# A two-layer decoder trunk: the second pair of gate and up columns computed conventionally

## The chip, the core and the metric

The kernel runs on one core of a Trainium2 chip. Its engines are called as the profile calls them: PE is TensorE (matmuls; PEld its weight loads), DVE is VectorE, ACT is ScalarE, POOL is GpSimd, SP is SyncE, which here only issues DMAs. The metric is the device time of one execution in microseconds; smaller is better.

## The reference

The input is 512 tokens of 1024 features in float32. Two layers run one after the other, each `x += 1/2 SwiGLU(RMSNorm(x)); x += Mixer(RMSNorm(x)); x += 1/2 SwiGLU(RMSNorm(x))`. The mixer of the first layer is pooling beside latent attention, that of the second a gated short convolution; the change doesn't touch them. The four SwiGLU half-steps are what it touches:

```python
def swiglu(x, w_gate, w_up, w_down):        # (512,1024) @ (1024,2816), twice; then @ (2816,1024)
    return (jax.nn.silu(x @ w_gate) * (x @ w_up)) @ w_down
```

## The kernel before

**Precision.** Activations and weights are split into a high and a low float32r part (`split`, lines 86 to 88: ACT casts the high part, DVE subtracts for the low one), and each product is three matmuls: high by high, high by low, low by high. Tiles `whi` and `wlo` hold the two parts of one weight chunk of 128 by 1024, each with three buffers; so the split of a chunk can be made when the matmuls on the third chunk before it are done.

**Layout.** Features lie in partitions, tokens in the free dimension. The 2816 hidden columns are 22 tiles of 128, taken as 11 pairs, numbered 0 to 10. A pair needs gate and up for two column tiles.

**Seven products.** Pairs 1 to 10 are computed by a Strassen-Winograd scheme on 2 by 2 blocks: two halves of the 1024 features by two halves of the 512 tokens on the activation's side. Instead of eight block products there are seven, P1 to P7, each of 24 matmuls 256 columns wide. Each product takes one combination of the weights, made by DMAs that add into a loaded tile (POOL's queue, tiles `sto` and `ar`; plain loads go through SP's queue), and one combination of the normalised input, a *factor*: `B11`, `T1`, `N2`, `B21`, `T3`, `N22`, `T4`. Pairs are computed in a staggered order, so that the P4 of one pair comes behind the P5 and P1 of the next. Their results sit in PSUM banks (six, tag `bank`), are copied or combined by ACT and DVE (`gate_up`), gated, and turned into blocks `hh` for the down projection, which also goes by seven products (`down`), in three groups of pairs.

**The start of a half-step.** The factors need the normalised input, and so the reciprocal norm R of each token, which is known late. Pair 0 is therefore computed conventionally from the input scaled by the gains alone, tile `xs`, and R is multiplied in afterwards. That is four chunks, each a `quarter` of 24 matmuls 512 columns wide. Between them the squares are summed over the partitions (`token_sums`, line 316), turned into R (`rsqrt`, DVE), spread over the partitions by matmuls (`norm_rows`, line 334) and copied by ACT (line 336). Then DVE makes the normalised tiles `xn` (line 379), DVE and ACT the seven factors (lines 382 to 405; the T4 is last), and behind them the gating of pair 0 (lines 453 to 464) and its blocks.

**What sets the order.** The text is written pair by pair, but a scheduler decides in which order the instructions stand in each engine's queue; within a queue an instruction waits for all ahead of it. Weight chunks are split three ahead of their use and loaded up to six ahead, through three buffers `raw`, through `sto` and `ar` (two each) for the summed ones.

Of the kernel before, what the change touches and what calls it, by code (L numbers as in the profile page):

```python
# [10 lines left out]
F32 = mybir.dt.float32  # L11
F32R = mybir.dt.float32r
AF = mybir.ActivationFunctionType
# [28 lines left out]
def trunk(ctx: ExitStack, tc: tile.TileContext, a, out):  # L42
# [21 lines left out]
    def bank(tag="bank", bufs=None):  # L64
        return pp.tile([P, 512], F32, tag=tag, name=tag, bufs=bufs)
# [101 lines left out]
    for l in range(2):  # L167
        for f in ("ffn1", "ffn2"):
            if f == "ffn2":
                if l == 0:  # L170
                    chunks += [Chunk(a["a_lat"][j], CH) for j in range(5)]
                    chunks += [Chunk(a["a_kr"], NK * DR)]
                    chunks += [Chunk(a["a_u"][j], CH) for j in reversed(range(4))]
                    chunks += [Chunk(a["a_w_out"][j, :, :CH // 2], CH // 2) for j in range(NK)]
                    chunks += [Chunk(a["a_w_out"][j, :, CH // 2:], CH // 2) for j in range(NK)]
                else:
                    for j in range(NK):
                        chunks += [Chunk(a["c_w_in"][s * NK + j], CH) for s in (1, 2, 0)]
                    chunks += [Chunk(a["c_w_out"][j], CH) for j in range(NK)]
            gu = a[f + "_w_gu"][l]  # L180
            turn = len(plans) + 1
            chunks += [Chunk(gu[0, q], CH) for q in (0, 2, 1, 3)]

            what = []
            for gi, (p0, p1) in enumerate(GROUPS):
                last = gi + 1 == len(GROUPS)
                what += [("gu", p) for p in range(max(p0, 1), p1 + 1 - last) if ("gu", p) not in what]
                what += [("down", (gi, e)) for e in range(2)]
            units = []
            for kind, p in what:  # L190
                if kind == "gu":
                    units.append(seven([gu[p, q] for q in range(4)], CH, turn))
                else:
                    gi, e = p
                    p0, p1 = GROUPS[gi]
                    n = 2 * (p1 - p0) * P
                    w = a[f"{f}_w_down{gi}"][l]
                    units.append(seven([w[e, q] for q in range(4)], n, turn))
            order = staggered([k for k, _ in what], max(j for j, (k, _) in enumerate(what) if k == "gu"))
            plans[l, f] = what, order  # L200
            chunks += [units[i][s] for i, s in order]
# [138 lines left out]
    def ffn(l, f, which, after, first=False):  # L340
        what, order = plans[l, f]
        with ExitStack() as es:
# [6 lines left out]
            def eight():  # L349
                return fp.tile([P, 8, HT], F32, tag="hz", name="hz")  # L350
# [17 lines left out]
            norm = lambda: rows.extend(norm_rows(norm_columns()))  # L368
            quarter(banks[2:4], 0, True, False, None if first else norm)
            if first:  # L370
                norm()
            R, Rp = rows
            with tc.tile_pool(name="np", bufs=1) as np_:
                xn = [np_.tile([P, 4, T], F32, tag=f"xn{e}", name=f"xn{e}") for e in range(2)]
# [29 lines left out]
                factor("N22", b22, -1.0)  # L404
                nc.vector.scalar_tensor_tensor(t1, t1, -1.0, b21, ALU.mult, ALU.subtract)
                factor("T4", t1)
            quarter(banks[0:2], 4, False, True)
            quarter(banks[2:4], 4, False, True)


# [7 lines left out]
            def put(p, names, src):  # L418

                j, c = home[p % 4][names[0]]  # L420
                j += 7 * (p // 4)
                if j not in four:
                    if j in (0, 1, 2, 7, 9, 10, 14):
                        t = hx.tile([P, 4 * T + 64], F32R, tag="hx", name="hh")[:, 48:48 + 4 * T]
                    else:
                        t = hy.tile([P, 4 * T], F32R, tag="hy", name="hh")
                    four[j] = t.rearrange("p (c f t) -> p c f t", c=2, f=4)
                v = four[j][:, :, c:c + len(names)]
                split(src, v[:, 0], v[:, 1])
                hfac.setdefault(p, {}).update({b: (v[:, 0, i], v[:, 1, i]) for i, b in enumerate(names)})  # L430
# [3 lines left out]
            def blocks(p, hz, rest):  # L434
# [11 lines left out]
                else:  # L446
                    nc.vector.scalar_tensor_tensor(hz[:, T4], hz[:, N2], -1.0, hz[:, B21], ALU.mult, ALU.subtract)
                    put(p, ("B21", "T4"), hz[:, B21:T4 + 1])


            hz = eight()
            for e in range(2):
                g, u = banks[2 * e:2 * e + 2]
                t = tp.tile([P, T], F32, tag="t", name="t")
                nc.vector.tensor_mul(t, g, R)  # L455
                nc.scalar.activation(t, t, AF.Silu)
                v = tp.tile([P, T], F32, tag="t", name="v")
                nc.vector.tensor_mul(v, u, R)
                if e == 0:
                    nc.vector.tensor_mul(hz[:, B11], v[:, :HT], t[:, :HT])  # L460
                    nc.vector.tensor_mul(hz[:, B12], v[:, HT:], t[:, HT:])
                else:
                    nc.vector.tensor_mul(hz[:, B21], v[:, :HT], t[:, :HT])
                    nc.vector.scalar_tensor_tensor(hz[:, N22], v[:, HT:], -1.0, t[:, HT:], ALU.mult, ALU.mult)


            live = {}
# [86 lines left out]

            for n, (i, s) in enumerate(order):
                if n == 3:
                    blocks(0, hz, False)
                    blocks(0, hz, True)
                kind, p = what[i]
                (gate_up if kind == "gu" else down)(i, p, s)  # L560

# [489 lines left out]
```

## Time and profile before

| | us |
|---|---|
| runs, median of 3 | 1764.47 |
| lowest and highest | 1763.59, 1764.65 |
| the profiled execution, its own time | 1768.79 |
| its span, first to last instruction | 1767.0 |
| PE busy | 1697.0 |
| DVE busy | 1328.1 |
| ACT busy | 906.9 |
| POOL busy | 312.0 |

The profiled execution is one more run, with the profiler on; its times start with its first instruction. The half-steps' conventional pairs end on PE at 40, 578, 928 and 1447 us. The mean granted clock of TensorE over the span is 0.985 of full speed.

### The profile page before, as it was taken

How to read it: one execution, taken by the hardware profiler on the slowest of the kernel's cores; microseconds unless marked ns; L12 is line 12 of the kernel's file. 1: busy time of each engine (PE TensorE's matmuls, PEld its weight loads, DVE VectorE, ACT ScalarE, POOL GpSimd, SP SyncE). 2: the span in 40 equal slices, each digit the busy share in tenths (PEclk: the TensorE clock that was granted, in tenths of full speed). 3: DMA queues.
4: the chain of work that ended last, by engine and by line, in shares of the span. 5: the costliest groups of instructions: out<-in, count | busy, mean ns of one | idle time of the engine just before them, and what ended most of it. 6: DMA issues, size and time to landing. Idle time of an engine off the chain costs nothing.

```text
span 1767.0 us, 31319 instructions
## 1 busy us (share of the span) xinstructions
PE 1697.0 (96%) x12642; PEld 1594.4 (90%) x12642; DVE 1328.1 (75%) x1891; ACT 906.9 (51%) x1300; POOL 312.0 (18%) x359
## 2 busy tenths in 40 slices
PE   7899999999999799999998999999999989999998
PEld 5799999978888799999988999999788879999998
DVE  6877786877896977677798777868755677867866
ACT  5654554564654554564556545545322345645553
POOL 2111111224202111111121111112100111111111
PEclk9999999998999899999999999999999999999999
DMA  6689888740015498889776899897322248988986
GB/s 215 157 209 215 216 211 212 165 142 24 19 42 173 106 214 218 213 206 217 173 194 153 208 219 223 207 212 164 108 96 96 96 133 194 222 216 209 218 210 138
DMA packets 89185, 303.19 MB, mean 172 GB/s; under 512 B 10704, under 2 KB 11472, under 8 KB 89040
## 3 DMA queue, kind: packets, MB, share of 16 engines
q0 software_dynamic: 36864, 130.04, 42.1%
q1 hardware_dynamic: 50512, 169.89, 27.2%
q8 instruction: 99, 1.62, 0.4%
q10 hardware_dynamic: 1664, 1.26, 0.2%
q14 instruction: 46, 0.38, 0.1%
HBM read 299.06 MB, written 2.10 MB: 170 GB/s over the span
## 4 chain that ended last, share of the span: by engine, by line
PE 80%; DVE 10%; issue 3%; ACT 3%; DMA 3%; POOL 1%; SPq 0%; ACTq 0%; DVEq 0%; POOLq 0%
PE bank L476 61%; PE bank L218 5%; PE bank L219 5%; PE bank L220 5%; DMA sto<-in_ffn_w_gu 2%; DVE wlo L88 2%; ACT whi L87 1%; DVE xn L379 1%; DVE xs L242 1%; DVE fT L88 1%; DVE fB L88 1%; PE bank L882 0%; PE held L218 0%; PE held L219 0%; PE held L220 0%
## 5 line engine op out<-in xcount | busy, mean ns | idle before, releaser
L476 PE MATMUL bank<-hh,whi 128*128 128x256 f32 x2464 | 429.9, 278 | 7.3 <-ACT whi L87 3.9
L476 PEld LDWEIGHTS bank<-hh,whi 128*128 128x128 f32 x2464 | 374.3, 188 | 10.4 <-ACT whi L87 4.9
L476 PE MATMUL bank<-fT,whi 128*128 128x256 f32 x1920 | 337.8, 279 | 8.5 <-ACT whi L87 2.9
L476 PE MATMUL bank<-hh,wlo 128*128 128x256 f32 x1232 | 341.5, 278 | 4.1 <-DVE wlo L88 4.1
L87 ACT CAST whi<-sto 128x1024 fp32r<-128x1024 f32 (+1 forms) x192 | 196.1, 1023 | 263.7 <-PE bank L476 164.4
L88 DVE TENSOR_TENSOR wlo<-sto,whi 128x1024 fp32r<-128x1024 f32 (+1 forms) x192 | 228.8, 1192 | 107.4 <-ACT whi L87 106.1
L476 PEld LDWEIGHTS bank<-fT,whi 128*128 128x128 f32 x1920 | 292.1, 189 | 11.2 <-ACT whi L87 3.5
L476 PE MATMUL bank<-fT,wlo 128*128 128x256 f32 x960 | 266.7, 278 | 0.0
L476 PE MATMUL bank<-fN,whi 128*128 128x256 f32 x1280 | 237.5, 288 | 14.4 <-ACT x L482 9.5
L476 PEld LDWEIGHTS bank<-hh,wlo 128*128 128x128 f32 x1232 | 231.0, 188 | 4.9 <-DVE wlo L88 4.9
L476 PE MATMUL bank<-fB,whi 128*128 128x256 f32 x1280 | 231.3, 280 | 4.2 <-DVE t L455 4.1
L476 PEld LDWEIGHTS bank<-fN,whi 128*128 128x128 f32 x1280 | 199.3, 193 | 25.3 <-ACT x L482 13.6
L87 ACT CAST whi<-a 128x1024 fp32r<-128x1024 f32 (+1 forms) x128 | 131.3, 1026 | 144.4 <-PE bank L476 88.1
L476 PEld LDWEIGHTS bank<-fB,whi 128*128 128x128 f32 x1280 | 197.8, 190 | 4.9 <-DVE t L455 4.9
L124 POOL DMA_DIRECT2D sto<-in_ffn_w_gu x120 | 104.6, 871 | 517.3 <-DVE wlo L88 294.9
L88 DVE TENSOR_TENSOR wlo<-a,whi 128x1024 fp32r<-128x1024 f32 (+1 forms) x128 | 152.3, 1190 | 53.3 <-ACT whi L87 53.0
L88 DVE TENSOR_TENSOR wlo<-ar,whi 128x1024 fp32r<-128x1024 f32 (+1 forms) x128 | 152.3, 1190 | 49.1 <-ACT whi L87 48.8
L87 ACT CAST whi<-ar 128x1024 fp32r<-128x1024 f32 (+1 forms) x128 | 130.9, 1022 | 112.2 <-PE bank L476 55.6
L476 PE MATMUL bank<-fN,wlo 128*128 128x256 f32 x640 | 181.3, 283 | 6.2 <-DVE wlo L88 6.2
L476 PE MATMUL bank<-fB,wlo 128*128 128x256 f32 x640 | 178.7, 279 | 5.5 <-DVE wlo L88 5.5
L476 PEld LDWEIGHTS bank<-fT,wlo 128*128 128x128 f32 x960 | 181.3, 189 | 0.0
L219 PE MATMUL bank<-xs,whi 128*128 128x512 f32 x392 | 154.9, 395 | 1.8 <-DVE xs L242 1.6
(242 smaller groups left out, 2877.9 us busy)
## 6 DMA issues: line engine op xcount, KB each, us to landing
sto<-in_ffn_w_gu POOLq DMA_DIRECT2D x120, 512.0 KB, 7.4
a<-in_ffn_w_gu SPq DMA_DIRECT2D x80, 512.0 KB, 6.5
sto<-in_ffn_w_down POOLq DMA_DIRECT2D x48, 512.0 KB, 7.7
sto<-in_ffn_w_gu SPq DMA_DIRECT2D x40, 512.0 KB, 4.2
ar<-in_ffn_w_gu SPq DMA_DIRECT2D x40, 512.0 KB, 5.4
ar<-in_ffn_w_gu POOLq DMA_DIRECT2D x40, 512.0 KB, 5.4
a<-in_ffn_w_down SPq DMA_DIRECT2D x32, 512.0 KB, 6.0
raw<-in_c_w_in SPq DMA_DIRECT2D x24, 512.0 KB, 3.4
```

The lines of the kernel that those rows point to most:

```text
L87: nc.scalar.copy(hi, raw)
L88: nc.vector.tensor_sub(lo, raw, hi.bitcast(F32))
L124: nc.gpsimd.dma_start(out=self.unit[tag], in_=self.srcs[q], accum_op=ALU.add)
L218: nc.tensor.matmul(ps, wh, ah, start=start, stop=False)
L219: nc.tensor.matmul(ps, wh, al, start=False, stop=False)
L220: nc.tensor.matmul(ps, wl, ah, start=False, stop=stop)
L242: nc.vector.scalar_tensor_tensor(xl, x[k], g, xh.bitcast(F32), ALU.mult, ALU.subtract)
L379: nc.vector.scalar_tensor_tensor(xn[e][:, i], x[k], gains[:, which, k:k + 1], R if e else Rp, ALU.mult, ALU.mult)
L476: nc.tensor.matmul(o, w_[:, s], a_, start=fresh and e == 0 and k == 0 and i == 0, stop=last and i == 2, skip_group_check=True)
```

## The change

Pair 1 is computed as pair 0 is: from the scaled input, conventionally, in four quarters. Its chunks are plain loads in the order of its two column tiles, so its first two quarters complete the first tile's gate and up, the last two the second's. In the text its quarters stand behind the gating of pair 0, and the blocks of pair 0 are made between them. The gating of pair 0 becomes a function, `first_h`, which serves both. The products begin with pair 2. Two smaller edits go along. In the first half-step the norm's steps move from behind the second quarter into the third, which for that goes ahead of the factors. And the hidden blocks of pairs 0 and 1 now live in pool `hy`, those of the next two in pool `hx`, since `hx` holds the scaled input for longer.

```diff
-            chunks += [Chunk(gu[0, q], CH) for q in (0, 2, 1, 3)]
+            chunks += [Chunk(gu[p, q], CH) for p in range(2) for q in ((0, 1, 2, 3) if p else (0, 2, 1, 3))]
...
-                what += [("gu", p) for p in range(max(p0, 1), p1 + 1 - last) if ("gu", p) not in what]
+                what += [("gu", p) for p in range(max(p0, 2), p1 + 1 - last) if ("gu", p) not in what]
...
             quarter(banks[2:4], 0, True, False, None if first else norm)
             if first:
-                norm()
+                quarter(banks[0:2], 4, False, True, norm)
...
-            quarter(banks[0:2], 4, False, True)
+            if not first:
+                quarter(banks[0:2], 4, False, True)
             quarter(banks[2:4], 4, False, True)
...
-                    if j in (0, 1, 2, 7, 9, 10, 14):
+                    if j in (4, 5, 6, 7, 9, 10, 14):
...
+            hz = first_h(banks)
+            pair1 = [bank() for _ in range(2)]
+            quarter(pair1[0:2], 0, True, False)
+            quarter(pair1[0:2], 4, False, True)
+            blocks(0, hz, False)
+            blocks(0, hz, True)
+            pair1 += [bank() for _ in range(2)]
+            quarter(pair1[2:4], 0, True, False)
+            quarter(pair1[2:4], 4, False, True)
+            hz = first_h(pair1)
...
                 if n == 3:
-                    blocks(0, hz, False)
-                    blocks(0, hz, True)
+                    blocks(1, hz, False)
+                    blocks(1, hz, True)
```

On DVE in the second half-step (the third looks the same) these rows stand around the last factor, `fT4`; `wlo` from `sto` or `a1` are low halves for products, `t`, `v` and `hz` belong to the gating of pair 0. Before:

```order
L88 TENSOR_TENSOR fT3_6296<-hz_6403,fT3_6296 128x1024
L405 SCALAR_TENSOR_TENSOR hz_6403<-hz_6403,xn1_6396 128x1024
L455 TENSOR_TENSOR t_6489<-bank_6299,R_6378 128x512
L458 TENSOR_TENSOR v_6492<-bank_6300,R_6378 128x512
L88 TENSOR_TENSOR fT4_6298<-hz_6403,fT4_6298 128x1024
L88 TENSOR_TENSOR wlo_6508<-sto_6303,whi_6507 128x1024
L460 TENSOR_TENSOR hz_6488<-v_6492,t_6489 128x256
L461 TENSOR_TENSOR hz_6488<-v_6492,t_6489 128x256
L88 TENSOR_TENSOR wlo_6538<-a1_6425,whi_6537 128x1024
```

And now, where `raw_6241` and `raw_6332` are the chunks of pair 1's third and fourth quarter:

```order
L88 TENSOR_TENSOR fT3_6204<-hz_6310,fT3_6204 128x1024
L405 SCALAR_TENSOR_TENSOR hz_6310<-hz_6310,xn1_6303 128x1024
L456 TENSOR_TENSOR t_6397<-bank_6207,R_6285 128x512
L459 TENSOR_TENSOR v_6400<-bank_6208,R_6285 128x512
L88 TENSOR_TENSOR fT4_6206<-hz_6310,fT4_6206 128x1024
L88 TENSOR_TENSOR wlo_6416<-raw_6241,whi_6415 128x1024
L461 TENSOR_TENSOR hz_6396<-v_6400,t_6397 128x256
L462 TENSOR_TENSOR hz_6396<-v_6400,t_6397 128x256
L88 TENSOR_TENSOR wlo_6444<-raw_6332,whi_6443 128x1024
```

The low halves for two products at that place gave way to those for the third and fourth quarter of pair 1; what stands ahead of them is as it was.

In the last half-step the place ahead of `fT4` differs; before:

```order
L88 TENSOR_TENSOR fT3_15397<-hz_15504,fT3_15397 128x1024
L405 SCALAR_TENSOR_TENSOR hz_15504<-hz_15504,xn1_15497 128x1024
L88 TENSOR_TENSOR wlo_15558<-ar_15407,whi_15557 128x1024
L455 TENSOR_TENSOR t_15590<-bank_15400,R_15479 128x512
L88 TENSOR_TENSOR fT4_15399<-hz_15504,fT4_15399 128x1024
L458 TENSOR_TENSOR v_15593<-bank_15401,R_15479 128x512
L88 TENSOR_TENSOR wlo_15609<-sto_15404,whi_15608 128x1024
L460 TENSOR_TENSOR hz_15589<-v_15593,t_15590 128x256
```

And now (`raw_15124` is pair 1's second quarter, `raw_15154` its third):

```order
L88 TENSOR_TENSOR fT3_15117<-hz_15223,fT3_15117 128x1024
L405 SCALAR_TENSOR_TENSOR hz_15223<-hz_15223,xn1_15216 128x1024
L88 TENSOR_TENSOR wlo_15279<-raw_15124,whi_15278 128x1024
L456 TENSOR_TENSOR t_15310<-bank_15120,R_15198 128x512
L88 TENSOR_TENSOR fT4_15119<-hz_15223,fT4_15119 128x1024
L459 TENSOR_TENSOR v_15313<-bank_15121,R_15198 128x512
L88 TENSOR_TENSOR wlo_15329<-raw_15154,whi_15328 128x1024
L461 TENSOR_TENSOR hz_15309<-v_15313,t_15310 128x256
```

Here it is the second quarter's low half that stands between the subtraction for T4 (line 405) and `fT4`, where a product's stood.

On PE in the first half-step the token sums (line 316) and the matmuls that spread R (line 334) stand elsewhere, among the wide matmuls of the third quarter; this is the difference, first for the sums:

```order
 L219 MATMUL bank<-xs_162,whi 128x512
 L220 MATMUL bank<-xs_162,wlo 128x512
+L316 MATMUL held<-ones,acc 128x2 x3
 L218 MATMUL bank<-xs_151,whi 128x512
 L219 MATMUL bank<-xs_151,whi 128x512
 L220 MATMUL bank<-xs_151,wlo 128x512
-L334 MATMUL held<-ident,rb 128x128 x4
 L218 MATMUL bank<-xs_151,whi 128x512
```

then for the spreading matmuls:

```order
 L218 MATMUL bank<-xs_162,whi 128x512
 L219 MATMUL bank<-xs_162,whi 128x512
+L334 MATMUL held<-ident,rb 128x128 x4
 L220 MATMUL bank<-xs_162,wlo 128x512
 L218 MATMUL bank<-xs_162,whi 128x512
```

The last three token sums moved behind twelve wide matmuls, and the spreading matmuls stand eight wide ones behind them.

## Rows read from the trace of the kernel before

**Rows 1.** The page's part 1: busy time, share of the span, instructions.

```profile
PE 1697.0 (96%) x12642; PEld 1594.4 (90%) x12642; DVE 1328.1 (75%) x1891; ACT 906.9 (51%) x1300; POOL 312.0 (18%) x359
```

**Rows 2.** Busy us and instructions by engine in three stretches; PEclk, DMA.

```profile
932.00:936.00 4.00, 1.70 (x14) 1.42 (x12) 4.00 (x5) 2.25 (x3) 0.00 (x0) 1.00 0.35 70
936.00:940.00 4.00, 1.43 (x6) 1.00 (x5) 4.00 (x6) 2.96 (x3) 0.00 (x0) 0.52 0.00 0
940.00:944.00 4.00, 4.00 (x25) 4.00 (x25) 4.00 (x7) 0.68 (x2) 0.87 (x1) 0.63 0.63 100
```

**Rows 3.** TensorE's timeline, half-step 1: start, us, line, tiles.

```profile
37.70 0.39 PE L218 MATMUL bank<-xs,whi 128*128 128x512 f32 x1
...
40.42 0.28 PE L476 MATMUL bank<-fT,whi 128*128 128x256 f32 x1
...
41.92 0.39 PE L476 MATMUL bank<-fT,whi 128*128 128x256 f32 x2
...
43.28 0.39 PE L476 MATMUL bank<-fT,whi 128*128 128x256 f32 x2
```

**Rows 4.** The same view where the first pair ends, half-steps 2 to 4.

```profile
577.30 0.39 PE L220 MATMUL bank<-xs,wlo 128*128 128x512 f32 x1
...
927.51 0.40 PE L476 MATMUL bank<-fT,whi 128*128 128x256 f32 x2
...
1446.50 0.40 PE L476 MATMUL bank<-fT,whi 128*128 128x256 f32 x2
```

**Rows 5.** VectorE's timeline, line 529 in the four half-steps.

```profile
119.42 0.42 DVE L529 SCALAR_TENSOR_TENSOR hz<-bank,c 128x256 f32<-128x256 f32 x1
...
662.15 0.42 DVE L529 SCALAR_TENSOR_TENSOR hz<-bank,c 128x256 f32<-128x256 f32 x1
...
963.55 0.42 DVE L529 SCALAR_TENSOR_TENSOR hz<-bank,c 128x256 f32<-128x256 f32 x1
...
984.65 0.42 DVE L529 SCALAR_TENSOR_TENSOR hz<-bank,c 128x256 f32<-128x256 f32 x1
...
1004.47 0.42 DVE L529 SCALAR_TENSOR_TENSOR hz<-bank,c 128x256 f32<-128x256 f32 x1
...
1524.68 0.42 DVE L529 SCALAR_TENSOR_TENSOR hz<-bank,c 128x256 f32<-128x256 f32 x1
```

**Rows 6.** VectorE's timeline: the first normalised tiles, two low halves behind them.

```profile
33.72 1.41 DVE L379 SCALAR_TENSOR_TENSOR xn<-x,gains,held 128x512 f32<-128x512 f32 x2 [2.02 <-ACT R L336]
...
574.11 1.40 DVE L379 SCALAR_TENSOR_TENSOR xn<-x,gains,held 128x512 f32<-128x512 f32 x2
...
918.11 1.41 DVE L379 SCALAR_TENSOR_TENSOR xn<-x,gains,held 128x512 f32<-128x512 f32 x2
...
938.23 1.22 DVE L88 TENSOR_TENSOR wlo<-sto,whi 128x1024 fp32r<-128x1024 f32 x1
...
1435.50 0.75 DVE L379 SCALAR_TENSOR_TENSOR xn<-x,gains,held 128x512 f32<-128x512 f32 x1 [1.93 <-ACT R L336]
...
1453.28 1.22 DVE L88 TENSOR_TENSOR wlo<-ar,whi 128x1024 fp32r<-128x1024 f32 x1
```

**Rows 7.** TensorE's timeline: the token sums, half-steps 1 and 4.

```profile
27.91 0.72 PE L316 MATMUL held<-ones,acc 128*128 128x2 f32 x6
...
1430.72 0.95 PE L316 MATMUL held<-ones,acc 128*128 128x2 f32 x8
```

**Rows 8.** Timelines of TensorE and ScalarE on the way to R, half-step 2.

```profile
566.42 1.05 PE L334 MATMUL held<-ident,rb 128*128 128x128 f32 x8
...
571.88 1.05 ACT L87 CAST whi<-sto 128x1024 fp32r<-128x1024 f32 x1 [8.44 <-DMA sto<-in_ffn_w_gu]
...
572.96 0.59 ACT L336 COPY R<-held 128x512 f32<-128x512 f32 x1
```

**Rows 9.** TensorE's waits: us in total, times, longest.

```profile
PE bank L476 <- ACT x L482: 11.2, 13, 3.2
```

**Rows 10.** The page's part 6: DMA issues, KB each, median us to landing.

```profile
sto<-in_ffn_w_gu POOLq DMA_DIRECT2D x120, 512.0 KB, 7.4
```

More of the change, by code (lines that the diff above doesn't have):

```diff
@@ L448, in blocks, with first_h @@
                     put(p, ("B21", "T4"), hz[:, B21:T4 + 1])
[L451 to L464, printed above, removed]
+            def first_h(banks):
+                hz = eight()
+                for e in range(2):
+                    g, u = banks[2 * e:2 * e + 2]
+                    t = tp.tile([P, T], F32, tag="t", name="t")
+                    nc.vector.tensor_mul(t, g, R)
+                    nc.scalar.activation(t, t, AF.Silu)
+                    v = tp.tile([P, T], F32, tag="t", name="v")
+                    nc.vector.tensor_mul(v, u, R)
+                    if e == 0:
+                        nc.vector.tensor_mul(hz[:, B11], v[:, :HT], t[:, :HT])
+                        nc.vector.tensor_mul(hz[:, B12], v[:, HT:], t[:, HT:])
+                    else:
+                        nc.vector.tensor_mul(hz[:, B21], v[:, :HT], t[:, :HT])
+                        nc.vector.scalar_tensor_tensor(hz[:, N22], v[:, HT:], -1.0, t[:, HT:], ALU.mult, ALU.mult)
+                return hz
+            hz = first_h(banks)
[8 more added lines that the diff above has]
+            hz = first_h(pair1)
             live = {}
```

## The prediction

> **What bounds the kernel now.** I read the page first. TensorE is busy for 96% of the span [rows 1], so what can be won is only what TensorE loses, and what a change adds to its work is paid in full unless it fills such a loss. The table of stretches then showed where it loses: not in the middle of the half-steps but just behind the four places where the conventional first pair ends and the first seven-product pair begins. There VectorE is busy without a break while TensorE stands, and after it has stood the granted clock drops to its lower level, 1.2 GHz: in the third half-step TensorE is busy for 1.70 and 1.43 us of two neighbouring stretches of 4 us, and the granted clock is 0.52 and then 0.63 in the stretches that follow [rows 2].
>
> The timeline of TensorE gives the size of its work. Twelve 512-wide matmuls of the conventional pair take 40.42 - 37.70 = 2.72 us, 0.2267 us each; twelve 256-wide ones of a product take 43.28 - 41.92 = 1.36 us, 0.1133 each [rows 3]. A pair computed conventionally is 96 wide matmuls, 21.76 us; by seven products it is 168 narrow ones, 19.04 us; one product is 2.72 us.
>
> Two marks per half-step measure the loss. E is where the conventional pair ends on TensorE: 40.42, 577.53 (the last start, 577.30, and one spacing), 927.51 and 1446.50 [rows 3, 4]. The other mark is VectorE's instruction on line 529, which comes once in a pair, behind its last product, P4. For the third pair computed by products it stands at 119.42, 662.15, 1004.47 and 1524.68 [rows 5]. From E to there it takes **79.00, 84.62, 76.96 and 78.18 us**. Bare work would be nine products to the first P4 (order: P5, P1, P6, P2, P7, next P5, P3, next P1, P4), 24.5 us, and twice 19.0 more: 62.6. So 14 to 22 us are lost each time.
>
> What is late is VectorE's chain that makes the factors. It begins with the normalised tiles, at a time that I call T0: 33.72, 574.11, 918.11, 1435.50 [rows 6]. In the third half-step the low half of T4 is done and the next weights' low half ends at 938.23 + 1.22 = 939.45, T0 + 21.3 [rows 6], while E was 9.4 us behind T0. TensorE has nothing to do for that time but the few products whose factors are ready.
>
> **The change part by part.** *Added work.* 21.76 - 19.04 = 2.72 us of TensorE in each half-step, 10.9 in all, certain.
>
> *Cover.* The 21.76 us of the second conventional pair stand between E and the first product. They need no factor, only the scaled input and weights. The cover ends where something else on VectorE is late, and the order shows what: the low half of the third quarter of the new pair stands behind the low half of T4. In the first three half-steps it ends at T0 + 21.3 (the same instructions in the same number stand ahead of it as ahead of the row at 938.23). TensorE wants it two quarters behind E, at E + 10.88. So TensorE waits 10.4 - (E - T0).
>
> - Half-step 1: three of four token sums move behind 12 more wide matmuls, 27.91 + 2.72 = 30.6, and from the sums to T0 it takes 1435.50 - 1430.72 = 4.8 us where nothing is in between [rows 6, 7], so T0 is 35.4. TensorE reaches the transposing matmuls 8 wide ones behind the sums, 1.8 us, and their operand comes some 1 us later (4.8 less the 1.05 and 0.6 of matmuls and copy is about 3): E becomes 41.4. The wait is 10.4 - 6.0 = 4.4 us.
> - Half-step 2: T0 was late, because the copy of R at 572.96 stood on ScalarE behind a cast whose summed weights landed only at 571.88, though the matmuls for it began at 566.42 [rows 8]. Now a plain load stands there. R follows the matmuls (1.05) and a cast, T0 becomes about 568.5, and the wait is 10.4 - 9.0 = 1.4. If the plain load lands no sooner than the summed one, T0 stays at 574.1 and the wait is 7.
> - Half-step 3: E - T0 is 9.4, the wait 1.0.
> - Half-step 4: here the order puts the second quarter's low half behind the subtraction for T4. That place is 1453.28 in the old trace, the operation ends at 1454.5 [rows 6], and TensorE wants it at E + 5.44 = 1451.9: wait 2.5.
>
> *Clock.* What TensorE does at the lower level costs the same time again. The nearest row is the third half-step's pair of waits [rows 2]: 1.43 x 0.48 + 4 x 0.37 = 2.2 us. No stall of the size of 1.0 to 1.4 has to do that. I take 2.2 for the wait of 4.4, 1.5 for that of 2.5, nothing for the others; the bounds are nothing, and 2.2 in each half-step for this wait and once more for the one that comes next.
>
> *The first product pair.* With all factors ready it still has waits of its own. P6 adds into the bank of P1, so ScalarE must first copy P1's result (the waits for that copy sum to 11.2 us over the kernel, the longest 3.2 [rows 9]). Ahead of that copy stands a cast into the buffer that P1 frees: 1.05 and 0.59 [rows 8], 1.7 us of TensorE. Then an estimated 1.7 us for the subtraction ahead of P3 and for the last cast and gating behind P4. From the end of the pair to line 529: 24.5 + 3.4 = 28 us. In half-steps 2 and 3 the summed weights of P6 come late as well: their accumulation is issued when P5's low half is made, by the order some 5 us behind the third quarter's, about T0 + 26, and takes 7.4 us to land [rows 10], so T0 + 33.4, 1.2 us later than the cast could begin: 29.2.
>
> *The second product pair*, then the third of all. Before, the pair behind the first one took 984.65 - 963.55 = 21.1 us, and the next 19.8 [rows 5]. I let the second one behind the start cost 21.1 now too.
>
> *Not on the path.* A pair less by products is three weight splits less on ScalarE and VectorE, four loads and four accumulations less. The hidden tiles change places between two pools of 4 and 5 buffers; each place is free when it is wanted, since the first pairs are used up some 16 us earlier than it is written again. I cost these at nothing.
>
> The sum, from the old E to the same mark (pair 3 of the half-step, counted from 0):
> - 1: 1.0 + 21.76 + 4.4 + 2.2 + 28 + 21.1 = 78.5; before 79.0; gain 0.5
> - 2: 21.76 + 1.4 + 29.2 + 21.1 = 73.5; before 84.6; gain 11.1
> - 3: 21.76 + 1.0 + 29.2 + 21.1 = 73.1; before 77.0; gain 3.9
> - 4: 21.76 + 2.5 + 1.5 + 28 + 21.1 = 74.9; before 78.2; gain 3.3
>
> Together 18.8 us. The profiled execution took 1768.79 us with a span of 1767.0, so it would become 1750.0; the median of the runs is 4.3 lower, 1764.47, and becomes **1745.7**; I say 1746. Bounds: with every wait and every drop of the clock gone (4.4, 1.4, 1.0, 2.5, 2.2, 1.5, 2.4 for the late P6, 1 at the start) 16.4 more is won, 1729. With the clock dropping twice in each half-step, 8 x 2.2 less the 3.7 counted, 13.9 is lost, 1760.
>
> **The rivals.**
>
> *The stall only moves.* VectorE's chain is not shortened by the change, it is given 21.76 us of cover, and it has the second pair's gating and the making of its blocks on top. If TensorE drops to its lower level at the new pair's third quarter and again at P1's copy in every half-step, the time is 1760; halfway 1753. For it: in the trace VectorE is busy for all of 4.00 us in each stretch around the stall [rows 2]. Against it: by my sum VectorE reaches the end of the first pair's blocks at T0 + 31, which in half-steps 2 and 3 is before the new pair ends.
>
> *Slower: the loads of the new pair are late.* Its fourth quarter is fetched on the SyncE queue behind loads for later products, into a buffer that the pair's first quarter frees. In half-step 4 that is about T0 + 10 = 1445; wanted is it about 16 us later. The accumulations take 7.4 us to land [rows 10]. It would have to land in over 20 us, in all four half-steps, to cost the 4.7 us each at which the gain is gone; at 8 us each the time is 1764.5 + 4 x 8 - 18.8 = 1778. Nothing in the trace is that slow; the start of half-step 2, where the old kernel waited for such a landing, is the place to watch.
>
> *Cheaper wide matmuls.* If 512 columns cost less than twice 256, the added work turns into a saving. At the extreme, 0.1133 each, the new pair would be 10.9 us instead of 21.76 and the time 1702. Against it: the spacings 0.2267 and 0.1133 stand in one stretch of one trace, in the ratio of the columns [rows 3]. The Trainium skill, "TensorE: Matmul & The Clock Gate", section "Back-to-back issue gap", would have it so: it gives a sustained 131 ns for 512 columns and 81 for 128, which by interpolation is an estimate of 98 for 256, so a pair of 12.6 us conventionally against 16.4 by products, and the sum would end near 1720. The trace does not agree: 227 and 113 ns.
>
> *No change:* the cover wins only what the wider pair costs, as in my half-step 1. If half-step 2 kept its late T0, and the clock fell everywhere, the rest is within 3 us of nothing.
>
> **How the numbers follow.** My forecast, 1738 to 1753: 0.60. The moved stall, 1753 to 1761: 0.16. More won, 1729 to 1738: 0.10. Below that, wide matmuls cheaper: 0.02. Within 0.2% (3.5 us, about what a measurement of this kernel can tell): 0.06. Late loads, slower: 0.06. The predicted time is that of the first. The range 1733 to 1760 takes in nearly all of the moved stall and half of the case of more won, and leaves out the other half, the cheaper matmuls, no change and late loads, together 0.2. Faster by over 0.2%: 0.88; within: 0.06; slower: 0.06.
>
> **What would show it.** Behind each E the wide matmuls should run on for another 21.8 us, with one wait for a low half: 4.4, 1.4, 1.0 us ahead of the third quarter in half-steps 1 to 3, 2.5 ahead of the second in half-step 4. T0 of half-step 2 should lie about 9 us ahead of E. The copy of P1's result should still be waited for, 1.7 to 3 us. From the end of the first conventional pair to the gating behind P4 of the fourth pair of a half-step (the third by products before, now the second; line 529, which becomes 542) I expect 78.5, 73.5, 73.1 and 74.9 us. I am wrong if the clock drops in more places than two, if VectorE is still at the first pair's blocks when the new pair ends, or if a load ends the wait instead of VectorE.

## The result, and the profile after

The changed kernel takes **1733.51 us** (median of 4 runs, 1731.38 to 1736.72); the kernel before, beside it on the same chip, 1764.03 (1761.19 to 1764.65). The ratio is 0.9839, 95% interval 0.9817 to 0.9861: 28 us faster by the ratio, 30.5 by the medians, where 18.5 were forecast. The profiled execution took 1735.6 us, its span is 1733.9 (1768.79 and 1767.0 before).

The page's part 1, beside [rows 1]:

```profile
PE 1692.3 (98%) x12354; PEld 1574.8 (91%) x12354; DVE 1312.8 (76%) x1883; ACT 889.7 (51%) x1268; POOL 299.2 (17%) x343
```

TensorE is busy for about as long as before, in a span that is 33 us shorter: what went is its idle time, from 70 us to 42. TensorE's waits of the whole run (total, times, longest) say which. The largest of the products' matmul, line 476, before:

```profile
PE bank L476 <- DVE wlo L88: 15.8, 8, 4.8
```

And after, where line 476 is line 489:

```profile
PE held L316 <- DVE acc L322: 6.8, 1, 6.8
PE bank L489 <- DVE wlo L88: 6.3, 6, 1.7
PE bank L489 <- ACT whi L87: 3.6, 5, 0.8
PE bank L220 <- DVE wlo L88: 3.1, 2, 1.5
PE bank L218 <- DVE t L456: 2.0, 1, 2.0
...
PE bank L489 <- ACT x L495: 0.7, 4, 0.2
```

The products' waits for low halves of weights (`wlo`) fall from 15.8 us to 6.3, those for ScalarE's copies of results, P1's among them (`x`), from 11.2 [rows 9] to 0.7. New are three waits inside the wide pair: two on line 220 for a low half of weights, and one on line 218 for a bank that VectorE's line 456 has yet to read. TensorE's timeline has them, and the four places where the first product pair begins:

```profile
52.78 0.39 PE L220 MATMUL bank<-xs,wlo 128*128 128x512 f32 x1
55.17 0.47 PE L218 MATMUL bank<-xs,whi 128*128 128x512 f32 x1 [2.01 <-DVE t L456]
...
57.95 0.80 PE L220 MATMUL bank<-xs,wlo 128*128 128x512 f32 x1 [1.54 <-DVE wlo L88]
...
69.50 0.40 PE L489 MATMUL bank<-fT,whi 128*128 128x256 f32 x2
...
591.25 0.40 PE L489 MATMUL bank<-fT,whi 128*128 128x256 f32 x2
...
925.61 0.40 PE L489 MATMUL bank<-fT,whi 128*128 128x256 f32 x2
...
1426.04 0.50 PE L220 MATMUL bank<-xs,wlo 128*128 128x512 f32 x1 [1.54 <-DVE wlo L88]
...
1441.63 0.40 PE L489 MATMUL bank<-fT,whi 128*128 128x256 f32 x2
```

Half-steps 2 and 3 run through the whole new pair without a wait. VectorE's timeline gives T0 in each half-step (line 379, beside [rows 6]) and the marks behind the first and the second product pair (line 542, which was 529 in [rows 5]; these are pairs 2 and 3 of the half-step):

```profile
36.56 2.72 DVE L379 SCALAR_TENSOR_TENSOR xn<-x,gains,held 128x512 f32<-128x512 f32 x4 [1.93 <-ACT R L336]
...
97.86 0.42 DVE L542 SCALAR_TENSOR_TENSOR hz<-bank,c 128x256 f32<-128x256 f32 x1
...
117.64 0.42 DVE L542 SCALAR_TENSOR_TENSOR hz<-bank,c 128x256 f32<-128x256 f32 x1
...
559.75 2.72 DVE L379 SCALAR_TENSOR_TENSOR xn<-x,gains,held 128x512 f32<-128x512 f32 x4
...
620.06 0.41 DVE L542 SCALAR_TENSOR_TENSOR hz<-bank,c 128x256 f32<-128x256 f32 x1
...
640.36 0.42 DVE L542 SCALAR_TENSOR_TENSOR hz<-bank,c 128x256 f32<-128x256 f32 x1
...
894.11 2.72 DVE L379 SCALAR_TENSOR_TENSOR xn<-x,gains,held 128x512 f32<-128x512 f32 x4
...
954.24 0.41 DVE L542 SCALAR_TENSOR_TENSOR hz<-bank,c 128x256 f32<-128x256 f32 x1
...
974.19 0.42 DVE L542 SCALAR_TENSOR_TENSOR hz<-bank,c 128x256 f32<-128x256 f32 x1
...
1406.99 2.72 DVE L379 SCALAR_TENSOR_TENSOR xn<-x,gains,held 128x512 f32<-128x512 f32 x4 [1.93 <-ACT R L336]
...
1469.92 0.42 DVE L542 SCALAR_TENSOR_TENSOR hz<-bank,c 128x256 f32<-128x256 f32 x1
...
1489.61 0.42 DVE L542 SCALAR_TENSOR_TENSOR hz<-bank,c 128x256 f32<-128x256 f32 x1
```

**Where the 33.1 us of span came from.** I cut the run at the first token sum of each later half-step (line 316; the fourth before is 1430.72 [rows 7]) and at the mark of pair 3. TensorE's timeline before, half-steps 2 and 3, then after, 2 to 4:

```profile
562.06 0.95 PE L316 MATMUL held<-ones,acc 128*128 128x2 f32 x8
...
912.05 0.95 PE L316 MATMUL held<-ones,acc 128*128 128x2 f32 x8
```

```profile
553.69 0.95 PE L316 MATMUL held<-ones,acc 128*128 128x2 f32 x8
...
888.04 0.95 PE L316 MATMUL held<-ones,acc 128*128 128x2 f32 x8
...
1402.20 0.95 PE L316 MATMUL held<-ones,acc 128*128 128x2 f32 x8
```

From the start of a half-step (in half-step 1 the start of the span) to that mark it took 119.42, 100.09, 92.42 and 93.96 us before, and 117.64, 86.67, 86.15 and 87.41 after: gains of 1.8, 13.4, 6.3 and 6.5, together **28.0**. The other 5.1 lie in work that the change doesn't touch: 4.3 in the mixer of layer 1 (from the last mark of half-step 1 to the token sums of half-step 2, 230.89 to 226.56), the rest in pieces of about 2 us and of both signs. The last section shows that both kinds come and go between executions.

The granted clock (fifth figure from the left, behind PE's busy time and count) drops in one place of the four, behind the two waits of half-step 1:

```profile
52.00:56.00 4.00, 1.99 (x9) 1.00 0.00 0
56.00:60.00 4.00, 2.46 (x7) 0.71 0.27 77
60.00:64.00 4.00, 4.00 (x17) 0.87 0.51 185
```

### The profile page after: what moved, and what is told of

Its sections match the earlier page's. It is cut to its first block, busy times and chain, and to the rows that moved or that the text cites. A ratio compares the mean times of both kernels' runs of the same rounds, so it can differ in the third digit from the quotient of the medians.

```text
span 1733.9 us, 30670 instructions
## 1 busy us (share of the span) xinstructions
PE 1692.3 (98%) x12354; PEld 1574.8 (91%) x12354; DVE 1312.8 (76%) x1883; ACT 889.7 (51%) x1268; POOL 299.2 (17%) x343
## 4 chain that ended last, share of the span: by engine, by line
PE 82%; DVE 9%; issue 4%; ACT 2%; DMA 2%; POOL 1%; SPq 0%; ACTq 0%; DVEq 0%; POOLq 0%
PE bank L489 59%; PE bank L220 6%; PE bank L218 6%; PE bank L219 6%; DVE wlo L88 2%; DMA sto<-in_ffn_w_down 1%; ACT whi L87 1%; DVE xn L379 1%; DMA sto<-in_ffn_w_gu 1%; PE bank L895 1%; DVE xs L242 1%; PE held L218 0%; PE held L219 0%; PE held L220 0%; DVE x L560 0%
## 5 line engine op out<-in xcount | busy, mean ns | idle before, releaser
L489 PE MATMUL bank<-fT,whi 128*128 128x256 f32 x1728 | 303.6, 278 | 0.0
L489 PEld LDWEIGHTS bank<-fT,whi 128*128 128x128 f32 x1728 | 262.2, 188 | 2.0 <-ACT x L495 1.5
L489 PE MATMUL bank<-fT,wlo 128*128 128x256 f32 x864 | 239.1, 278 | 0.0
L489 PE MATMUL bank<-fN,whi 128*128 128x256 f32 x1152 | 208.3, 283 | 3.5 <-ACT x L495 0.7
L218 PE MATMUL bank<-xs,whi 128*128 128x512 f32 x520 | 206.0, 397 | 2.5 <-DVE t L456 2.0
L220 PE MATMUL bank<-xs,wlo 128*128 128x512 f32 x520 | 204.4, 394 | 3.2 <-DVE wlo L88 3.1
L219 PE MATMUL bank<-xs,whi 128*128 128x512 f32 x520 | 204.9, 394 | 1.8 <-DVE xs L242 1.5
L489 PE MATMUL bank<-fB,whi 128*128 128x256 f32 x1152 | 205.9, 278 | 0.0
L489 PEld LDWEIGHTS bank<-fN,whi 128*128 128x128 f32 x1152 | 174.2, 188 | 13.8 <-DVE c L532 8.4
L489 PEld LDWEIGHTS bank<-fB,whi 128*128 128x128 f32 x1152 | 176.3, 188 | 0.0
L87 ACT CAST whi<-raw 128x1024 fp32r<-128x1024 f32 (+2 forms) x91 | 86.9, 958 | 163.6 <-PE bank L219 143.1
```

The lines of the kernel that those rows point to most:

```text
L87: nc.scalar.copy(hi, raw)
L218: nc.tensor.matmul(ps, wh, ah, start=start, stop=False)
L219: nc.tensor.matmul(ps, wh, al, start=False, stop=False)
L220: nc.tensor.matmul(ps, wl, ah, start=False, stop=stop)
L489: nc.tensor.matmul(o, w_[:, s], a_, start=fresh and e == 0 and k == 0 and i == 0, stop=last and i == 2, skip_group_check=True)
```

## The experiments

My theory: TensorE stood still behind the first conventional pair because VectorE's chain of factors was not done; the second conventional pair covers the chain, and costs 2.72 us more of TensorE. The rivals: the gain is fewer weight splits and loads, wherever they stand; or the moved norm, or the changed places of the hidden tiles, do it. Each kernel ran beside the kernel before on its chip, so ratios are compared. The four numbers of the table are those just used, from the start of the half-step to the mark of pair 3.

| kernel | half-step 1 | 2 | 3 | 4 | median, us | ratio to before, 95% |
|---|---|---|---|---|---|---|
| before | 119.42 | 100.09 | 92.42 | 93.96 | 1764.03 | |
| changed | 117.64 | 86.67 | 86.15 | 87.41 | 1733.51 | 0.9839 (0.9817 to 0.9861) |
| changed, again | 117.57 | 86.44 | 85.80 | 87.60 | 1738.41 | 0.9855 (0.9832 to 0.9878) |
| 1: half-step 2 alone | 119.73 | 85.86 | 94.28 | 92.33 | 1749.86 | 0.9929 (0.9917 to 0.9941) |
| 2: before, short chain | 111.29 | 91.85 | 84.14 | 89.42 | 1731.88 | 0.9838 (0.9824 to 0.9853) |
| 3: changed, short chain | 110.32 | 85.28 | 85.57 | 85.90 | 1724.77 | 0.9795 (0.9780 to 0.9810) |
| 4: third wide pair | 118.81 | 87.52 | 87.59 | 89.38 | 1739.41 | 0.9870 (0.9856 to 0.9885) |
| 5: loads held | 125.03 | 96.49 | 96.42 | 95.41 | 1765.88 | 1.0031 (1.0018 to 1.0044) |
| 6: norm put back | 113.17 | 86.09 | 86.06 | 87.39 | 1730.14 | 0.9818 (0.9802 to 0.9834) |
| 6, again | 112.48 | 85.92 | 85.79 | 88.00 | 1733.23 | 0.9836 (0.9814 to 0.9858) |
| 7: places put back | 117.40 | 86.41 | 86.39 | 87.80 | 1734.75 | 0.9850 (0.9832 to 0.9869) |
| 8: norm back, T4 later | 113.14 | 85.90 | 85.91 | 86.37 | 1728.33 | 0.9819 (0.9804 to 0.9834) |

**1. The change in half-step 2 alone.**

```diff
-            chunks += [Chunk(gu[p, q], CH) for p in range(2) for q in ((0, 1, 2, 3) if p else (0, 2, 1, 3))]
+            wide = 2 if (l, f) == (0, "ffn2") else 1
+            chunks += [Chunk(gu[p, q], CH) for p in range(wide) for q in ((0, 1, 2, 3) if p else (0, 2, 1, 3))]
...
+            if wide2:
                 pair1 = [bank() for _ in range(2)]
...
                 hz = first_h(pair1)
```

> The kernel before with the second conventional pair in half-step 2 alone; the other three half-steps, the norm's place and their pools as before. My theory (what is gained is the stall behind the end of the first pair in each half-step, largest in half-step 2): 13 to 18 us faster than before, about 1748, with the third mark of the second half-step some 13 to 20 us earlier relative to the end of its first pair and nothing gained in half-steps 1, 3 and 4. Rival (the gain is less loading and splitting altogether): a quarter of the 30.5 us, 1756.

Measured: 0.9929, 12.2 us by the medians. The stretch of half-step 2 lost 14.2 us, the others changed by +0.3, +1.9 and -1.6. The place is as my theory has it; a quarter of the whole gain, 7.6, is not what one half-step gave. The size is at the low end, or by the medians just under it.

**2 and 3. The chain made shorter, in both kernels.** ScalarE makes the high half of each factor as before, VectorE's low halves are left out.

```diff
-                    if sign > 0:
-                        split(v, hi, lo)
-                    else:
-                        nc.scalar.mul(hi, v, -1.0)
-                        nc.vector.scalar_tensor_tensor(lo, v, -1.0, hi.bitcast(F32), ALU.mult, ALU.subtract)
+                    nc.scalar.mul(hi, v, sign)
...
-                    product(ps, e, w, [(b[:, 0, k], b[:, 1, k]) for k in range(4)], s in ("P1", "P5", "P2"))
+                    product(ps, e, w, [(b[:, 0, k], b[:, 0, k]) for k in range(4)], s in ("P1", "P5", "P2"))
```

> The kernel before without the low halves of the seven factors of the normalised input: the products use the high half twice, so TensorE has the same matmuls, but VectorE's chain loses seven operations of 1.14 us in each half-step. Left out of the computation are these low halves. My theory (TensorE waits for VectorE's chain behind the first pair): nearly all of the 8.0 us comes off each half-step, unless ScalarE's casts, which make the high halves, become what is late; 20 to 32 us in all, 1732 to 1744, and the second product pair, 20.5, 21.6, 21.1 and 19.5 us in the four half-steps of before, falls towards 19.8 because nothing is left over behind the chain. Rival (the changed kernel gains by fewer loads and splits, not by covering the chain): a little, 1755 to 1763.

> The changed kernel without the low halves of the seven factors of the normalised input, as in its twin made from the kernel before; the computation leaves out the same. My theory: the chain is covered already, so only the waits that are left in the new pair can go, 5.4 us in half-step 1, 1.9 in half-step 4, 0.3 in the others, 8 us at the most: 1726 to 1731. The gap between the twins falls from 30.5 us to 15 or less. Rival (the chain is not the cause): both twins gain the same, and the gap stays near 30.

Measured: the kernel before gains 28.1 us with TensorE's matmuls, all loads and all weight splits as they were. By half-step 8.1, 8.2, 8.3 and 4.5 us. That the total is near what the change gave is chance, since the change gave 1.8, 13.4, 6.3 and 6.5. The changed kernel gains 8 to 11 (0.9795 for 0.9839 and 0.9855; 7.3, 1.4, 0.6 and 1.5 in its stretches), somewhat more than I allowed, and between 40 and 70 us none of its waits on lines 218 and 220 is left. The gap between the twins is 7.1 us where it was 30.5. This is what tells the theories apart, and most of the gain falls to the chain.

The gap that is left isn't spread evenly: by the table, so in the two profiled executions, it is 1.0, 6.6, -1.4 and 3.5 us in the four half-steps. In half-step 2 the short chain still begins late. ScalarE's timeline has the cast of summed weights ahead of R's copy there, as in [rows 8]:

```profile
557.06 1.05 ACT L87 CAST whi<-sto 128x1024 fp32r<-128x1024 f32 x1 [8.54 <-DMA sto<-in_ffn_w_gu]
558.13 0.59 ACT L336 COPY R<-held 128x512 f32<-128x512 f32 x1
```

So T0 comes 12.1 us behind the token sums in both kernels made the old way (574.11 for 562.06; 559.28 for 547.13), and 6.1 in the changed one (559.75 for 553.69). By these numbers some 6 of the 13.4 us that the change gains in half-step 2 go to this earlier start of the chain, by the plain load in the summed one's place, and the rest to the cover; no run here has the one without the other. What the 3.5 us of half-step 4 are is open but for the wait shown below. One part of the expectation failed: the second product pair, 20.53, 21.58, 21.10 and 19.48 us before, fell to 19.8 in half-step 3 alone: it took 20.03, 20.57, 19.81 and 21.06. In half-step 4, where the least was gained, TensorE waits there for VectorE's sum behind P7:

```profile
PE bank L472 <- DVE c L515: 1.1, 1, 1.1
```

**4. A third conventional pair** in every half-step, where nothing is left to cover.

```diff
...
+            pair2 = [bank() for _ in range(2)]
+            quarter(pair2[0:2], 0, True, False)
+            quarter(pair2[0:2], 4, False, True)
+            blocks(1, hz, False)
+            blocks(1, hz, True)
+            pair2 += [bank() for _ in range(2)]
+            quarter(pair2[2:4], 0, True, False)
+            quarter(pair2[2:4], 4, False, True)
+            hz = first_h(pair2)
...
```

> The changed kernel with a third pair of gate and up computed conventionally in every half-step. My theory: the chain of the factors is covered by the second pair already, so the third covers nothing and only costs its longer TensorE work, 21.8 us for 19.9 of a product pair, less the 1 to 2 us of waiting that may be left: 1.9 in each half-step, 7.5 in all, 1741. Rival (fewer products mean less splitting and loading and that is what gained): as fast as the changed kernel or faster, 1725 to 1733.

Measured: 0.9870, 5.5 us above the changed kernel's 0.9839 and 2.6 above its second 0.9855, though the intervals overlap; by the marks 1.2, 0.9, 1.4 and 2.0, together 5.4, and 5.9 against the second trace. It has still fewer splits and loads than the changed kernel, and that does not pay for its wider matmuls. Of the 7.5 expected 1.2 came back in the first product pair: from its first matmul to its mark it takes 28.24, 28.16, 28.26 and 28.25 us, where the changed kernel has 28.36, 28.81, 28.63 and 28.29.

**5. The first loads of the product pairs held** until the last factor is made.

```diff
+            if tag and now[2]:
+                nc.gpsimd.tensor_copy(t[:, :1], now[2].pop())
             nc.sync.dma_start(out=t[:, :self.n], in_=self.srcs[q])
...
-            turn = len(plans) + 1
+            turn = 2 * len(plans) + 2
...
+            now[0] += 1
+            now[2] = 4 * [fac["T4"][:, 1, 0, :1].bitcast(F32)]
             quarter(pair1[2:4], 0, True, False)
```

> The changed kernel with the first four stored loads of the product pairs in each half-step held until the last factor of the normalised input is made, by a small copy from that factor into the tile ahead of the load. It tests whether the early landing of these loads behind the wide pair is what made the second product pair cheaper than I forecast (19.9 us for 21.1) and kept the first at 28.5. My theory: the first product pair waits for its weights then, its load landing some 7 us later than the factor; 2 to 5 us in each half-step, 8 to 20 us in all, 1741 to 1753. Rival (loads have slack behind the pair's 20 us anyway): no change, 1733.5.

The edit does one thing more than that: by `turn` and `now[0]` every load of a product pair, held or not, stands in the program behind the new pair's first two quarters. So what is measured is the lateness of all these loads.

Measured: 1.0031, 31 to 34 us above the changed kernel's two ratios; 7.4, 9.8, 10.3 and 8.0 by the marks. So late loads cost more than I expected, enough to eat the whole gain. The timelines of SyncE's queue, GpSimd's queue, VectorE and TensorE in half-step 2 show the way:

```profile
589.12 0.33 SPq L122 DMA_DIRECT2D sto<-in_ffn_w_gu  x1
...
593.27 0.93 POOL L126 DMA_DIRECT2D sto<-in_ffn_w_gu  x1 [2.37 <-DMA sto<-in_ffn_w_gu]
...
604.31 1.23 DVE L88 TENSOR_TENSOR wlo<-sto,whi 128x1024 fp32r<-128x1024 f32 x1 [6.86 <-ACT whi L87]
...
604.34 0.80 PE L493 MATMUL bank<-fT,whi 128*128 128x256 f32 x2 [4.93 <-ACT whi L87]
```

The last factor is done at 587.9 (586.68 + 1.23), the load is issued at 589.12, the accumulation into it at 593.27, and TensorE starts at 604.34, when the cast of the high half is done: two trips and a cast, 16 us, not the 7 that I had taken. In the changed kernel the same load is issued at 548.63 and its accumulation at 554.13. My guess on the second product pair fell here: with the loads held it still takes 19.85, 19.85, 19.83 and 19.71 us. All that they cost lies ahead of the first mark.

**6. The norm of half-step 1 put back**, then again beside the unchanged kernel.

```diff
-                quarter(banks[0:2], 4, False, True, norm)
+                norm()
...
-            if not first:
-                quarter(banks[0:2], 4, False, True)
+            quarter(banks[0:2], 4, False, True)
```

> The changed kernel with the norm of half-step 1 put back in front of the third quarter, so only that one move is undone. My theory (TensorE waits for the factors' chain, which begins at T0 on VectorE): in half-step 1 the normalised tiles begin 2.8 us earlier than in the changed kernel (33.7 for 36.56), TensorE's end of the first conventional pair comes back to 40.4 (42.3), the new pair ends between 1.9 and 2.8 us earlier, and the end of the program follows: 1731 where the changed kernel has 1733.5, the other three half-steps unchanged. Rival (the norm's move was needed to cover the chain): the wait in the new pair grows by the 1.9 that the end of the first pair moves, and the time stays at 1733.5 or above.

> The changed kernel once more, unchanged, beside the next kernel on the same chip. In the one execution that I read, its first half-step began its token sums at 32.0, in three other kernels with the same first 60 us at 30.1 to 30.3; I expect 30.3 here and the mark of the third product of the half-step's pairs at 116 to 117.6. Time 0.984 of before.

> The changed kernel with the norm of half-step 1 put back, once more, beside the changed kernel on the same chip. My theory (the norm's move delays T0 and the end of the first pair and by that the wait behind them): the mark at 113.2 again, 3 to 4.5 us faster than the changed kernel, 0.982 of before. Rival (its 1730 was the scatter of executions): within 1.5 us of the changed kernel.

Measured: 0.9818 and 0.9836, 3.7 us below the changed kernel in the first comparison and 3.3 in the second, each smaller than its interval; the stretch of half-step 1 is 4.4 to 5.2 us shorter in every pairing of the four traces, the others stay within 0.8. That part of the change costs time. It is more than the 1.9 to 2.8 expected, and the clock, which falls behind the waits in the changed kernel, is part of the difference. Another part may be the order on VectorE, which the edit changes too: with the norm put back one low half of the new pair stands ahead of T4's (52.74, then 53.87), in the changed kernel none does there (T4's at 55.54, the next at 56.68). No run here separates the two. With the norm put back TensorE waits 0.89 and 0.40 us, and the granted clock stays at its upper level, 2.4 GHz, in the same stretches:

```profile
52.00:56.00 4.00, 3.23 (x13) 1.00 0.23 74
56.00:60.00 4.00, 4.00 (x19) 1.00 0.51 188
```

The changed kernel's second trace has T0 at 35.43 and its mark at 117.57; the waits are 2.01 and 1.54 again. Its median is 1738.41, above 1733.51, with runs from 1732.6 to 1745.4.

**7. The old places of the hidden tiles**, (0, 1, 2, 7, 9, 10, 14) for (4, 5, 6, 7, 9, 10, 14).

> The changed kernel with the old list of the hidden tiles that live in the first of the two pools, so the change of places is undone. My theory (each place is free before it is wanted): no change, 1733.5, or a wait of VectorE or ScalarE for a place that TensorE does not feel. Rival (the new list is needed, because the first group's tiles live longer now that two pairs stand in front): TensorE waits for a split of hidden tiles in each half-step, 2 us or more each, 1741 or above.

Measured: 0.9850, in the interval of both runs of the changed kernel; the stretches differ from the first run's by 0.4 at most. No cost or gain of the places shows.

**8. The norm put back, and T4 written behind the new pair's first quarter.**

```diff
...
+                quarter(banks[0:2], 4, False, True)
+                quarter(banks[2:4], 4, False, True)
+                pair1 = [bank() for _ in range(2)]
+                quarter(pair1[0:2], 0, True, False)
                 nc.vector.scalar_tensor_tensor(t1, t1, -1.0, b21, ALU.mult, ALU.subtract)
                 factor("T4", t1)
-            if not first:
-                quarter(banks[0:2], 4, False, True)
-            quarter(banks[2:4], 4, False, True)
...
             hz = first_h(banks)
-            pair1 = [bank() for _ in range(2)]
-            quarter(pair1[0:2], 0, True, False)
             quarter(pair1[0:2], 4, False, True)
```

> The changed kernel with the norm of half-step 1 back in front of the third quarter, and with the last factor, T4, written in the program behind the new pair's first quarter, so that the order puts one more low half of the new pair's weights ahead of it on VectorE. My theory (what is left of waiting in the new pair is this low half behind T4): the 1.8 us that half-step 1 still loses there with the norm put back, and the 1.9 of half-step 4, fall to 0.5 or less each; with the 4.8 us that the norm alone gave at the start, about 8 us less than the changed kernel on the same chip, 1726. Rival (the wait then comes from the next operation of the chain): as with the norm alone, 1730.

Measured: 0.9819, no better than the norm alone. In half-step 4 the wait for the low half falls from 1.5 to 0.4 and the stretch by 1.0. In half-step 1 the rival was right: the low half is early now, and the bank is late, because VectorE reads it (line 457) behind T4's subtraction:

```profile
54.05 0.47 PE L218 MATMUL bank<-xs,whi 128*128 128x512 f32 x1 [2.03 <-DVE t L457]
```

The fastest versions are this one and the changed kernel with the norm put back, 0.982 of before; they are not told apart.

## Why the prediction was right, and where its sum was off

The mechanism is the one forecast, in both its parts: the cover, and the earlier T0 of half-step 2. Experiment 1 puts the gain in the half-step that is changed, 2 and 3 tie most of it to VectorE's chain, and 4 shows that relief of loads and splits does not pay by itself. The time is 12.5 us below the number, and inside the range by 0.5 us only: it fell where the prediction had put 0.10, into the case of more won, and not into its own 1738 to 1753. The second measurement, 0.9855, is 1738 us on the same scale, at the edge between the two. So it was partly luck that the time came inside. By the marks the four starts gave 28.0 us where the sum had 18.8. Where the 9.2 are, term by term:

- **E and T0 of half-step 1** (41.4 and 35.4 forecast). The wait for the bank stands 48 wide matmuls, 10.88 us, behind E, and the last of them starts at 52.78, so E is 52.78 + 0.23 - 10.88 = 42.13, and T0 36.56; in the second trace 51.64 + 0.23 - 10.88 = 40.99 and 35.43. The term was right; the profiled execution merely began its token sums 1.1 later. It makes the sum 0.7 longer.
- **Waits and clock in the new pair.** E of the other half-steps lies as far behind the token sums as before (15.47, 15.46, 15.78): 569.16, 903.50, 1417.98. From E to the first product, less 21.76, TensorE lost 5.6, 0.3, 0.4 and 1.9 us, where I had 6.6, 1.4, 1.0 and 4.0: **4.8 too much**. In half-step 1 the waits were 2.01 and 1.54 for 4.4, and the first of them was for a bank, which I had not named; the remaining 2.0 or so is the clock, for 2.2. In half-step 4 the wait was 1.54 for 2.5, and the clock did not drop, for which I had set 1.5. Low halves are wanted later than I counted: TensorE runs four matmuls of high halves ahead of the first that needs a low one.
- **T0 of half-step 2**, the largest single claim, came 9.4 us ahead of E, where 9 were forecast; the late summed load is gone from R's way. This was a start of the chain 6 us earlier, not cover, and experiments 2 and 3 find 6.6 us of difference there.
- **The first product pair**, 28, 29.2, 29.2 and 28 forecast: from its first matmul to its mark 28.36, 28.81, 28.63 and 28.29. The totals fit and the parts don't. The sum has 1.7 us for the copy of P1's result, and a wait of 1.7 to 3 us for it was named as a sign; the longest wait for such a copy is 0.2. Instead the nine products run in 25.8 to 26.3 us where 24.5 were counted, with listed waits of 0.5 at most, and the mark comes 2.4 to 2.5 behind them. That this term came out is luck.
- **The second product pair** was mis-sized: 21.1 forecast from one row of before, measured 19.78, 20.30, 19.95 and 19.69, **4.7 less** over the four. Of that 1.7 is the one row taken for all four: they took 20.53, 21.58, 21.10 and 19.48 before. In the kernel before TensorE still waits in it for ScalarE's copies and VectorE's sums, 1.3, 1.7, 1.3 and 0.2 us; in the changed kernel the trace has no wait in these four stretches. Early loads are not the reason (experiment 5). A shorter chain alone did not do it either (experiment 2), so which work ahead of those copies and sums had been late stays open.

One reading was off without weight: in [rows 2] the clock of 0.52 stands in the second of the two stretches with waits, not behind both.

Of the rivals, the stall with a drop of the clock did move in half-step 1, and there alone; the loads of the new pair were never late, but experiment 5 shows that the kind of price was real; the wide matmuls were no cheaper, 0.227 us each in the new pair too (52.10 to 52.78 in three spacings), and experiment 4 shows what an uncovered pair costs. (The Trainium skill, "TensorE: Matmul & The Clock Gate", section "Back-to-back issue gap", gives 131 ns for 512 columns; the traces here have 227.)

## What to carry to other kernels

When a chain on one engine delays the bound engine at the start of a stage, independent work of the bound engine in front of it may be dearer than the form it replaces and still win: here 2.72 us paid for 9 to 16 recovered in half-steps 2 to 4 (some 6 of the 16 by an earlier start of the chain), and the next such piece, with nothing to recover, cost 1.4. Make the covered chain shorter in both kernels: as far as the gap between them closes, the chain was the cause, and what is left of it is worth a look stage by stage: here the largest piece was another effect. Don't move the start of the chain later to fit the cover in: the moved norm, with the order that came of it, gave back 3 to 5 us.

## What was unexpected of the hardware

**A stretch that nobody changed scatters by 4.5 us.** The mixer of layer 1 took 230.89 us before and 226.56 after; in the other traces 226.4 to 230.6, and the same kernel (6) took 230.52 once and 226.60 the second time. The granted clock is the difference; here the stretches of the kernel before, with PE, PEld, DVE, ACT and POOL busy ahead of it,

```profile
400.00:405.00 5.00, 5.00 (x23) 4.40 (x22) 2.50 (x8) 2.70 (x15) 1.27 (x4) 0.66 0.21 54
...
435.00:440.00 5.00, 4.14 (x15) 3.69 (x16) 3.22 (x5) 2.17 (x4) 4.66 (x8) 0.50 0.32 105
```

and of the changed one:

```profile
400.00:410.00 10.00, 10.00 (x53) 9.20 (x52) 8.77 (x25) 4.83 (x9) 3.11 (x6) 1.00 0.01 2
...
430.00:440.00 10.00, 9.85 (x53) 8.14 (x54) 8.73 (x23) 5.70 (x13) 8.46 (x14) 1.00 0.14 47
```

So 4.3 of the 33.1 us between two profiles belong to no change, and a comparison stage by stage is worth more than one of spans.

**Like stretches of matmuls have two paces at the full granted clock.** A stretch between two marks that holds a group's down projection, 21 products of 24 matmuls, took 57.35 us in half-step 1 of the changed kernel (first group), and 59.31 in half-step 3 (second group; PE busy and its recorded matmuls, then the granted clock, 1.00 in both):

```profile
137.67:195.02 57.35, 57.21 (x502) 1.00 0.92 220
1111.84:1171.15 59.31, 59.27 (x504) 1.00 0.88 207
```

The slow pace turns up in other half-steps of other traces, in the kernel before in half-steps 1 and 2; what sets it is open.

**One wait of 2 us did not lower the clock; two close together did.** In experiment 8 TensorE stood still for 2.03 us up to 54.05, and the granted clock stays at 1.00 (fifth figure):

```profile
52.00:56.00 4.00, 1.97 (x10) 1.00 0.37 131
56.00:60.00 4.00, 4.00 (x19) 1.00 0.38 131
```

In the changed kernel it stood for 2.01, ran four matmuls and stood for 1.54, and the clock fell to its lower level, 1.2 GHz. The other four traces with these two waits, of the changed kernel again and of experiments 4, 5 and 7, have 0.50 from 56 to 60 us. I had priced the clock by the length of the waits alone.
